# Moving weight tiles by 64 bytes in SBUF: a wider pad at the right-hand edge and an offset inside the low-part tiles

## The chip, the cores and the metric

One core of a Trainium2 chip runs the whole layer in one launch. The time is the device time of one execution in microseconds (us), the median of several runs. Single instructions are in nanoseconds (ns). The engines are PE (TensorE, matmuls), PEld (its weight loads), DVE (VectorE), ACT (ScalarE), POOL (GpSimd) and SP (SyncE, which issues the large DMAs).

## The reference, cut to what matters

The kernel computes one decoder layer in float32 for 256 tokens of width 2048:

```python
h = rmsnorm(x, g_pre_mix)
proj = h @ w_in                                   # 2048 x 15376
oa = gated_deltanet(conv_silu(aq, ak, av), beta, logdecay) -> gated norm
ob = hgrn2(bq, bf, bi) -> gated norm
oc = memory_attention(cq, rmsnorm(mem, g_mem), w_kv_mem)
merged = sum_b sigmoid(gate_b) * (o_b @ w_br_b)
x = x + rmsnorm(merged @ w_out, g_post_mix)
m = square(relu(rmsnorm(x, g_pre_mlp) @ w_mlp_in)) @ w_mlp_out     # 2048 -> 8192 -> 2048
x = x + rmsnorm(m, g_post_mlp)
```

Nearly all of the work is dense products of 256 tokens with large weight matrices, and every weight is read from HBM once.

## The kernel before, in words

**Split products.** PE multiplies in a reduced form of float32 (type fp32r). To keep the accuracy, each operand is split into a high part (the value rounded to fp32r) and a low part (what is left). A product is then high x high, high x low and low x high. ACT makes the high part of a weight tile (`A.copy` into `wh` or `oh`), DVE the low part (a subtraction into `wl` or `ol`); this is `split_w`, lines 204 to 213. Activations are split once and kept: `hh` and `h2h` hold high and low side by side, `memT`, `mgh`/`mgl`, `och`/`ocl`, `mh`/`ml`, `sh`/`sl` likewise.

**A weight tile** is 128 x 2 x 512 elements of 4 bytes (`KG` = 2 blocks of 128 rows, 512 columns), 4096 bytes of each partition. A DMA on SP's queue brings it into a raw tile (`w`, or `raw` in the MLP), and ACT and DVE split it.

**Two ways to multiply.** A matmul has a stationary operand, which a weight load (LDWEIGHTS) brings into the array, and a moving operand, which streams through.

- In `unit` the activations are stationary (128 tokens) and the weights move, 512 columns at a time: three matmuls of 512 columns for each block of 128 rows and each half of the tokens. `first_unit` and the seven products of `seven` work in the same way. In the profile the weights stand first in such rows: `mm<-wh,hh`, `mm<-wl,hh`, `mm<-oh,mh`.
- In `unit_joined` and `unit_stacked` the weights are stationary, 128 columns at a time, and the activations move: for the high weights 512 columns (high and low of 256 tokens side by side), here called wide, and for the low weights 256 columns, here called narrow. `products_joined` issues them: the wide ones of two weight groups, then the narrow ones of the same groups, the order turned from one pair of groups to the next. So runs of wide and narrow follow one another. In the profile the activations stand first: `mm<-hh,wh` and `mm<-h2h,oh` (wide), `mm<-hh,wl` and `mm<-h2h,ol` (narrow).

**Stages.** The mixing stage (memory keys and values, input projection, three branches, output projection) uses both ways. Small steps of the recurrences run in between: `tick` pulls them from a list of generators (`bg`) after each group, so runs of equal matmuls are broken by small ones. The MLP goes over eight blocks `e` of 1024 hidden features: `mlp_in(e)` multiplies with the weights stationary (except the first unit), `mlp_out(e-1)` with the weights moving.

**The order of the work** on an engine is that of the code; the tile framework adds the waits. Nothing in the placement of a tile changes that order, except that a tile waits for the earlier users of the bytes that it takes.

**Where tiles lie.** Pools are laid from the left end of a partition or, with `side="right"`, from the right end. On the left lie the constants, the activations (`hp` and the 4096-byte slots `gp`) and, once the mixing stage is over, the pool `wx` with the MLP's operand pairs 0 and 1 (`oh0`, `ol0`, `oh1`, `ol1`) and `raw0`. On the right lie a pad named `edge`, which no instruction touches, and below it the pool `wp` (four tiles each of `w`, `wh`, `wl`); in the MLP the pool `wy` takes its place with `raw1` to `raw4` and the pairs 2 to 5. The MLP's six operand pairs are a ring: `operand` takes the first of the list and puts it at the end.

In the compiled kernel before, the start addresses are, in bytes within a partition:

```
hh, h2h            18304 + n * 8192    0 modulo 128
gp slots           51072 + n * 4096    0 modulo 128
wx: oh0 ... raw0  155008 + n * 4096    0 modulo 128   (n = 0..4)
wp: w             180160 + n * 4096   64 modulo 128   (n = 0..3)
wp: wh            196544 + n * 4096   64 modulo 128
wp: wl            212928 + n * 4096   64 modulo 128
wy: raw1 ... ol5  180160 + n * 4096   64 modulo 128   (n = 0..11)
```

Slices of these tiles start at multiples of 512 bytes, so the start modulo 128 of a tile is that of all its operands. It is called the phase below.

Of the kernel before, what the change touches and what calls it, by code (L numbers as in the profile page):

```python
# [10 lines left out]
F32 = mybir.dt.float32  # L11
F32R = mybir.dt.float32r
# [5 lines left out]
P = 128  # L18
# [15 lines left out]
KG = 2  # L34
# [6 lines left out]
def tile_trunk(ctx: ExitStack, tc, a):  # L41
# [39 lines left out]
    mk = mixing.enter_context(tc.tile_pool(name="mk", bufs=1))  # L81
    lp = mixing.enter_context(tc.tile_pool(name="lp", bufs=1))
    edge = ctx.enter_context(tc.tile_pool(name="edge", bufs=1, side="right"))
    edge.tile([P, 8], F32, tag="edge", name="edge")
    weights = ctx.enter_context(ExitStack())
    wp = weights.enter_context(tc.tile_pool(name="wp", bufs=4, side="right"))

# [2 lines left out]
    def nm(s):  # L90
        cnt[0] += 1
        return f"{s}_{cnt[0]}"

    def g4(name, shape=(P, 1024), dt=F32):
        return gp.tile(list(shape), dt, tag="g", name=nm(name))
# [99 lines left out]
    def load_w_raw(src, k0, n, c0, width=512, step=None, q=lambda i: i):  # L195
        w = wp.tile([P, KG, 512], F32, tag="w", name=nm("w"), bufs=WB)
        for j in range(0, n, step or n):
            m = min(step or n, n - j)
            q(nc.sync.dma_start(
                w[:, j:j + m, 0:width],  # L200
                src[(k0 + j) * P:(k0 + j + m) * P, c0:c0 + width].rearrange("(k p) n -> p k n", p=P),
            ))
        return w

    def split_w(w, n, width=512, step=None, q=lambda i: i, home=None):
        wh = home("wh") if home else wp.tile([P, KG, 512], F32R, tag="wh", name=nm("wh"))
        wl = home("wl") if home else wp.tile([P, KG, 512], F32R, tag="wl", name=nm("wl"))
        for j in range(0, n, step or n):
            js = slice(j, min(j + (step or n), n))
            q(A.copy(wh[:, js, 0:width], w[:, js, 0:width]))  # L210
            q(V.tensor_tensor(out=wl[:, js, 0:width], in0=w[:, js, 0:width],
                              in1=wh.bitcast(F32)[:, js, 0:width], op=ALU.subtract))
        return wh, wl

    def load_w(src, k0, n, c0, width=512, home=None):
        return split_w(load_w_raw(src, k0, n, c0, width), n, width, home=home)

    def unit(act, nk, src, c0, r0=0, order=None, split=False, post=None, ws=None, load=None):

# [49 lines left out]
    def unit_stacked(pairs, nk, src, c0, ps, load, ws):  # L269

        for gg in range(0, nk // KG, 2):
            groups = []
            for g in (gg, gg + 1):
                k0 = g * KG
                groups.append((k0, ws[g] if g in ws else load(src, k0, c0),
                               [flat(pairs[kt // 4][:, kt % 4]) for kt in range(k0, k0 + KG)]))
            for i, _ in enumerate(products_joined(ps, groups, nk, range(4), gg // 2 % 2)):
                tick(0.5)
# [4 lines left out]
    def unit_joined(both_of, src, c0):  # L283


        out = g4("sum", (P, 4, S))
        tiles, ps, ws = [], [], {}
        for i, (gs, h, turned) in enumerate(halved):
            if i in (0, 1):
                tiles.append(pmm.tile([P, 1024], F32, tag="mm", name=nm("mm")))  # L290
                ps.extend((tiles[-1][:, 0:512], tiles[-1][:, 512:1024]))
            for g in gs:
                if g not in ws:
                    ws[g] = load_w(src, g * KG, KG, c0)
            groups = [(g * KG, ws[g], [flat(both_of(kt)) for kt in range(g * KG, g * KG + KG)]) for g in gs]
            for _ in products_joined(ps, groups, KT, range(4) if h is None else (2 * h, 2 * h + 1), turned):
                tick(0.5 if h is None else 0.25)
            if 7 in gs:
                o = out[:, 2 * h:2 * h + 2, :]
                p = tiles[h].rearrange("p (c s n) -> p c s n", c=2, s=2)  # L300
                A.copy(o, p[:, :, 1, :])
                V.tensor_tensor(out=o, in0=p[:, :, 0, :], in1=o, op=ALU.add)
        return out
# [70 lines left out]
    def first_unit(src, c0):  # L374


        both = pmm.tile([P, 1024], F32, tag="mm", name=nm("mm"))
        ng = KT // KG
        ws, sw = {}, {}

        def fetch(g):
            load_mem(g)
            ws[g] = load_w_raw(src, g * KG, KG, c0, step=1 if g < 2 else None, q=pin)

        def piece(g, js, q=lambda i: i):
            if g not in sw:
                sw[g] = tuple(wp.tile([P, KG, 512], F32R, tag=t, name=nm(t)) for t in ("wh", "wl"))
            wh, wl = sw[g]
            q(A.copy(wh[:, js, :], ws[g][:, js, :]))
            q(V.tensor_tensor(out=wl[:, js, :], in0=ws[g][:, js, :], in1=wh.bitcast(F32)[:, js, :], op=ALU.subtract))  # L390

        def turn(g):
            parts = []
            for kt in (g * KG, g * KG + 1):
                pt, kk = bank("tr"), kt % 4
                for t in range(NT):
                    pin(T.transpose(pt[:, t * P:(t + 1) * P], mem_s[g // 2][:, t, kk * P:(kk + 1) * P], ident))
                parts.append((pt[:, 0:S], *mem_act(kt), gcol[:, kt:kt + 1]))
            return parts

        def products(kt):
            ah, al = mem_act(kt)
            wh, wl = sw[kt // KG]
            j = kt % KG
            ts = [slice(t * P, (t + 1) * P) for t in range(NT)]
            os = [both[:, t * 512:(t + 1) * 512] for t in range(NT)]
            for o, t in zip(os, ts):
                pin(T.matmul(o, ah[:, t], wh[:, j, :], start=kt == 0, stop=False))
                pin(T.matmul(o, al[:, t], wh[:, j, :], start=False, stop=False))
            for o, t in zip(os, ts):  # L410
                pin(T.matmul(o, ah[:, t], wl[:, j, :], start=False, stop=kt == KT - 1))

        fetch(0)
        fetch(1)
        idle_turns(11)
        turn_grow(grow_mem, 16, 0, pin)
        split_scaled(turn(0), pin)
        idle_turns(8)
        for j in range(KG):
            piece(0, slice(j, j + 1), pin)  # L420
        for g in range(ng):
            if 1 <= g < ng - 1:
                piece(g + 1, slice(0, KG))
            if g + 2 < ng:
                fetch(g + 2)
            products(g * KG)
            if g == 0:
                for j, part in enumerate(turn(1)):
                    split_scaled([part], pin)
                    piece(1, slice(j, j + 1), pin)  # L430
            elif g + 1 < ng:
                split_scaled(turn(g + 1))
            products(g * KG + 1)
            if g % 2 == 0 and g > 0:
                sumsq_chunk(mem_s[g // 2 - 1], ssm, g // 2 - 1)
            tick()
        sumsq_chunk(mem_s[3], ssm, 3)
        return both
# [185 lines left out]
    for u in range(2):  # L624
        k = unit_joined(lambda kt: memB[kt // 2][:, kt % 2], w_kv, 512 * u)
# [664 lines left out]
    for hg in range(2):  # L1290
        k, g = forget(unit_joined(hboth, w_in, OFF_BF + 512 * hg), hg)
# [76 lines left out]
    ahead = {}  # L1368

    def first_weights(ps):  # L1370
        for g in range(2):
            ahead[g] = load_w(a["w_mlp_in"][0], g * KG, KG, 0, home=lambda n: g4(n, (P, KG, 512), F32R))

    for c in range(4):
        ys.append(g4("y1", (P, NT, 512)))
# [37 lines left out]
    def at(pool, tag, dt):  # L1413
        return pool.tile([P, KG, 512], dt, tag=tag, name=tag, bufs=1)

    def pair_at(pool, i):
        return (at(pool, f"oh{i}", F32R), at(pool, f"ol{i}", F32R))

    pairs = [pair_at(wx, i) for i in range(2)]
    raws = [at(wx, "raw0", F32)]  # L1420
# [1 line left out]
    def wide_ring():  # L1422
        for g in range(2):
            w = load_w_raw(a["w_mlp_in"][0], g * KG, KG, 512)
            ahead[8 + g] = split_w(w, KG, home=operand)
        weights.close()
        wy = ctx.enter_context(tc.tile_pool(name="wy", bufs=1, side="right", reuse_waits="tile"))
        raws.extend(at(wy, f"raw{i}", F32) for i in range(1, 5))
        raws.append(g4("raw5", (P, KG, 512)))
        pairs.extend(pair_at(wy, i) for i in range(2, 6))  # L1430

    def operand(n):
        if n == "wh":
            pairs.append(pairs.pop(0))
        return pairs[-1][n == "wl"]

    def raw(src, k0, c0):
        w = raws.pop(0)
        raws.append(w)
        nc.sync.dma_start(w, src[k0 * P:(k0 + KG) * P, c0:c0 + 512].rearrange("(k p) n -> p k n", p=P))  # L1440
        return w

    def load_in(src, k0, c0):
        return split_w(raw(src, k0, c0), KG, home=operand)

    h2act = act_of(h2T)
    stf = const("stf", [P, 8])
# [240 lines left out]
```

## Time and profile before

| | |
|---|---|
| median of 3 runs | 1791.68 us (1791.08 to 1791.91) |
| profiled execution, its own time | 1793.1 us |
| span of the profiled execution | 1791.4 us |
| granted TensorE clock | 0.999 |
| PE busy in the span | 1777.5 us, 99% |
| DVE, ACT busy | 1303.3 us (73%), 960.6 us (54%) |
| HBM read | 356.86 MB, mean 203 GB/s moved |

How to read it: matmuls are pipelined, and the profile models their ends. The mean of one matmul (390 to 400 ns at 512 columns) is therefore not the time it adds. What it adds is the distance from its start to the start of the next, here called the pace. In a view in order of time, a row of n equal matmuls gives the start of the first and the time from there to the end of the last.

### The profile page before, as it was taken

What the parts mean: (1) busy time and instruction counts of PE and PEld (TensorE: products, weight loads), DVE (VectorE), ACT (ScalarE), POOL (GpSimd) and SP (SyncE); (2) the same over time, 40 slices, a digit from 0 to 9 for tenths busy, and PEclk for the clock granted to TensorE, in tenths of its full rate; (3) what the DMA queues carried; (4) which work ended last, traced back from release to release, by engine and by line L of the source; (5) the groups of instructions that cost most, each with busy time, mean ns of one, the idle gap of its engine ahead of it and who ended that gap; (6) DMA issues with size and microseconds to landing.
All of it is one profiled execution on the core that took longest, in us unless ns stands there. A gap on an engine that the chain in (4) does not pass through costs nothing.

```text
span 1791.4 us, 23962 instructions
## 1 busy us (share of the span) xinstructions
PE 1777.5 (99%) x9053; PEld 1493.9 (83%) x9053; DVE 1303.3 (73%) x1764; ACT 960.6 (54%) x1217; POOL 57.8 (3%) x100
## 2 busy tenths in 40 slices
PE   9999999999999999999999999999999999999998
PEld 7888888888888888888888888888888878888886
DVE  5765768684758487697555557796979797969795
ACT  6644665454555475565444445665545464645453
POOL 0000000400030000000000000000000000000000
PEclk9999999999999999999999999999999999999999
DMA  8665555875487465555566675776767676767683
GB/s 262 213 191 165 168 159 166 214 215 159 157 213 210 132 189 164 158 171 169 185 186 189 232 222 196 229 243 217 238 222 253 208 242 214 256 200 248 210 296 139
DMA packets 188804, 362.84 MB, mean 203 GB/s; under 512 B 14456, under 2 KB 16272, under 8 KB 188304
## 3 DMA queue, kind: packets, MB, share of 16 engines
q1 hardware_dynamic: 181856, 351.32, 62.0%
q0 software_dynamic: 2304, 5.44, 1.5%
q10 hardware_dynamic: 4528, 4.54, 0.9%
q8 instruction: 71, 1.16, 0.3%
q14 instruction: 45, 0.37, 0.1%
HBM read 356.86 MB, written 4.39 MB: 202 GB/s over the span
## 4 chain that ended last, share of the span: by engine, by line
PE 82%; DVE 2%; issue 1%; ACT 0%; DMA 0%; DVEq 0%; POOLq 0%; POOL 0%
PE mm L56 77%; DVE ol L56 1%; PE pa L56 1%; PE kk L56 0%; DVE relu L56 0%; PE bo L56 0%; PE o L56 0%; DMA raw<-in_w_mlp_out 0%; PE pzt L56 0%; PE pw L56 0%; PE tr L56 0%; DVE raw L56 0%; DVE ml L56 0%; PE y L56 0%; PE mgT L56 0%
## 5 line engine op out<-in xcount | busy, mean ns | idle before, releaser
L56 DVE TENSOR_TENSOR wl<-w,wh 128x1024 fp32r<-128x1024 f32 (+1 forms) x362 | 437.0, 1217 | 245.7 <-ACT wh L56 223.5
L56 ACT CAST wh<-w 128x1024 fp32r<-128x1024 f32 (+1 forms) x362 | 374.6, 1046 | 365.5 <-PE mm L56 296.0
L56 ACT CAST oh<-raw 128x1024 fp32r<-128x1024 f32 x288 | 299.0, 1051 | 283.0 <-PE mm L56 213.0
L56 DVE TENSOR_TENSOR ol<-raw,oh 128x1024 fp32r<-128x1024 f32 x288 | 343.4, 1221 | 100.8 <-ACT oh L56 68.0
L56 PE MATMUL mm<-wh,hh 128*128 128x512 f32 x1152 | 369.2, 395 | 0.0
L56 PEld LDWEIGHTS mm<-wh,hh 128*128 128x128 f32 x1152 | 216.3, 188 | 46.3 <-ACT wh L56 0.2
L56 PE MATMUL mm<-h2h,oh 128*128 128x512 f32 x960 | 228.4, 393 | 0.0
L56 PE MATMUL mm<-wl,hh 128*128 128x512 f32 x576 | 225.5, 392 | 0.0
L56 PEld LDWEIGHTS mm<-h2h,oh 128*128 128x128 f32 x960 | 177.9, 188 | 39.8
L56 PE MATMUL mm<-hh,wh 128*128 128x512 f32 x768 | 188.7, 396 | 0.7 <-ACT z L56 0.7
L56 PEld LDWEIGHTS mm<-hh,wh 128*128 128x128 f32 x768 | 140.7, 188 | 31.5 <-ACT z L56 0.9
L56 PE MATMUL mm<-oh,mh 128*128 128x512 f32 x372 | 146.6, 394 | 0.0
L56 PE MATMUL mm<-ol,mh 128*128 128x512 f32 x372 | 145.3, 391 | 1.1 <-DVE ol L56 1.0
L56 PE MATMUL mm<-oh,ml 128*128 128x512 f32 x372 | 144.9, 392 | 0.0
L56 PEld LDWEIGHTS mm<-wl,hh 128*128 128x128 f32 x576 | 108.3, 188 | 22.7
L56 PEld LDWEIGHTS mm<-h2h,ol 128*128 128x128 f32 x960 | 117.4, 190 | 3.2 <-DVE ol L56 0.6
L56 PE MATMUL mm<-h2h,ol 128*128 128x256 f32 x960 | 118.6, 281 | 0.4 <-DVE ol L56 0.4
L56 PEld LDWEIGHTS mm<-hh,wl 128*128 128x128 f32 x768 | 95.6, 188 | 4.0
L56 PE MATMUL mm<-hh,wl 128*128 128x256 f32 x768 | 98.0, 278 | 0.0
L56 PEld LDWEIGHTS mm<-ol,mh 128*128 128x128 f32 x372 | 69.8, 188 | 18.1 <-DVE ol L56 2.8
L56 PEld LDWEIGHTS mm<-oh,mh 128*128 128x128 f32 x372 | 69.9, 188 | 15.9 <-DVE acc L56 1.4
L56 PEld LDWEIGHTS mm<-oh,ml 128*128 128x128 f32 x372 | 69.8, 188 | 15.7
(363 smaller groups left out, 2212.7 us busy)
## 6 DMA issues: line engine op xcount, KB each, us to landing
w<-in_w_in SPq DMA_DIRECT2D x240, 512.0 KB, 4.2
raw<-in_w_mlp_out SPq DMA_DIRECT2D x170, 512.0 KB, 4.7
raw<-in_w_mlp_in SPq DMA_DIRECT2D x118, 512.0 KB, 4.8
w<-in_w_out SPq DMA_DIRECT2D x32, 512.0 KB, 4.4
w<-in_w_kv_mem SPq DMA_DIRECT2D x30, 512.0 KB, 5.0
w<-in_w_br_c SPq DMA_DIRECT2D x16, 512.0 KB, 3.8
w<-in_w_br_a SPq DMA_DIRECT2D x16, 512.0 KB, 4.5
w<-in_w_br_b SPq DMA_DIRECT2D x16, 512.0 KB, 3.6
```

The costliest lines, as they stand in the source:

```text
L56: ins = op(*args, **kwargs)
```

## The change

Three edits. The pad at the right-hand edge becomes 96 bytes instead of 32, so that everything on the right lies 64 bytes lower. The tiles for the low parts of weights (`wl` in `wp`, `ol0` to `ol5` in the MLP) become 128 bytes longer (32 elements). And a new helper `low` gives the 4096 bytes that are used in such a tile: from its start, or, with `aside=True`, from 64 bytes on. `aside` is set where the weights are stationary (`unit_joined`, and `unit_stacked` with the two groups loaded ahead for it); where the weights move, the low part starts at the tile's start. `home` now gives both tiles in one call, and `operand` turns the ring once for both, as before. No instruction is added or removed.

```diff
-    edge.tile([P, 8], F32, tag="edge", name="edge")
+    edge.tile([P, 24], F32, tag="edge", name="edge")
...
-    def split_w(w, n, width=512, step=None, q=lambda i: i, home=None):
-        wh = home("wh") if home else wp.tile([P, KG, 512], F32R, tag="wh", name=nm("wh"))
-        wl = home("wl") if home else wp.tile([P, KG, 512], F32R, tag="wl", name=nm("wl"))
+    def low(t, aside):
+        o = 16 if aside else 0
+        return t[:, o:o + KG * 512].rearrange("p (k n) -> p k n", k=KG)
+
+    def split_w(w, n, width=512, step=None, q=lambda i: i, home=None, aside=False):
+        if home:
+            wh, wl = home(aside)
+        else:
+            wh = wp.tile([P, KG, 512], F32R, tag="wh", name=nm("wh"))
+            wl = low(wp.tile([P, KG * 512 + 32], F32R, tag="wl", name=nm("wl")), aside)
...
-                groups.append((k0, ws[g] if g in ws else load(src, k0, c0),
+                groups.append((k0, ws[g] if g in ws else load(src, k0, c0, True),
...
-                    ws[g] = load_w(src, g * KG, KG, c0)
+                    ws[g] = load_w(src, g * KG, KG, c0, aside=True)
...
     def pair_at(pool, i):
-        return (at(pool, f"oh{i}", F32R), at(pool, f"ol{i}", F32R))
+        return at(pool, f"oh{i}", F32R), pool.tile([P, KG * 512 + 32], F32R, tag=f"ol{i}", name=f"ol{i}", bufs=1)
...
-            ahead[8 + g] = split_w(w, KG, home=operand)
+            ahead[8 + g] = split_w(w, KG, home=operand, aside=True)
...
-    def operand(n):
-        if n == "wh":
-            pairs.append(pairs.pop(0))
-        return pairs[-1][n == "wl"]
+    def operand(aside):
+        pairs.append(pairs.pop(0))
+        return pairs[-1][0], low(pairs[-1][1], aside)
```

More of the change, by code (lines that the diff above doesn't have):

```diff
@@ L213, in split_w, with load_w @@
         return wh, wl
-    def load_w(src, k0, n, c0, width=512, home=None):
-        return split_w(load_w_raw(src, k0, n, c0, width), n, width, home=home)
+    def load_w(src, k0, n, c0, width=512, home=None, aside=False):
+        return split_w(load_w_raw(src, k0, n, c0, width), n, width, home=home, aside=aside)
     def unit(act, nk, src, c0, r0=0, order=None, split=False, post=None, ws=None, load=None):
@@ L386, in piece @@
             if g not in sw:
-                sw[g] = tuple(wp.tile([P, KG, 512], F32R, tag=t, name=nm(t)) for t in ("wh", "wl"))
+                sw[g] = (wp.tile([P, KG, 512], F32R, tag="wh", name=nm("wh")),
+                         low(wp.tile([P, KG * 512 + 32], F32R, tag="wl", name=nm("wl")), False))
             wh, wl = sw[g]
@@ L1371, in first_weights @@
         for g in range(2):
-            ahead[g] = load_w(a["w_mlp_in"][0], g * KG, KG, 0, home=lambda n: g4(n, (P, KG, 512), F32R))
+            ahead[g] = load_w(a["w_mlp_in"][0], g * KG, KG, 0,
+                              home=lambda aside: tuple(g4(n, (P, KG, 512), F32R) for n in ("wh", "wl")))
     for c in range(4):
@@ L1441, in raw, with load_in @@
         return w
-    def load_in(src, k0, c0):
-        return split_w(raw(src, k0, c0), KG, home=operand)
+    def load_in(src, k0, c0, aside=False):
+        return split_w(raw(src, k0, c0), KG, home=operand, aside=aside)
     h2act = act_of(h2T)
```

## The prediction

> **What bounds the kernel now.** I read the page first: who is busy, and which chain ended last.
>
> ```profile
> span 1791.4 us, 23962 instructions
> PE 1777.5 (99%) x9053; PEld 1493.9 (83%) x9053; DVE 1303.3 (73%) x1764; ACT 960.6 (54%) x1217; POOL 57.8 (3%) x100
> ...
> PE   9999999999999999999999999999999999999998
> ...
> PEclk9999999999999999999999999999999999999999
> ```
>
> PE is busy from end to end at full clock, so the time is the number of matmuls times their pace. The change touches no count, only addresses; the question is whether the pace depends on them. Next I read the groups, for the counts of what reads a weight tile:
>
> ```profile
> L56 PE MATMUL mm<-wh,hh 128*128 128x512 f32 x1152 | 369.2, 395 | 0.0
> L56 PE MATMUL mm<-h2h,oh 128*128 128x512 f32 x960 | 228.4, 393 | 0.0
> L56 PE MATMUL mm<-wl,hh 128*128 128x512 f32 x576 | 225.5, 392 | 0.0
> L56 PE MATMUL mm<-hh,wh 128*128 128x512 f32 x768 | 188.7, 396 | 0.7 <-ACT z L56 0.7
> L56 PE MATMUL mm<-oh,mh 128*128 128x512 f32 x372 | 146.6, 394 | 0.0
> ...
> L56 PE MATMUL mm<-h2h,ol 128*128 128x256 f32 x960 | 118.6, 281 | 0.4 <-DVE ol L56 0.4
> L56 PE MATMUL mm<-hh,wl 128*128 128x256 f32 x768 | 98.0, 278 | 0.0
> ...
> L56 PE MATMUL mm<-oh,sh 128*128 128x512 f32 x112 | 45.0, 402 | 0.1
> ...
> L56 PE MATMUL mm<-memT,wh 128*128 128x512 f32 x128 | 31.7, 398 | 0.0
> ```
>
> The kernel before holds its own comparison. In the MLP, pairs 0 and 1 lie in `wx` at phase 0 (modulo 128 bytes, like the activations), pairs 2 to 5 in `wy` at phase 64, and the ring sends the same work through all six. The view in order of time shows one stretch of `mlp_in`; following the ring through the code, the 32 wide from 1139.72 all use pairs 2 to 5, the first 16 from 1150.93 pairs 0 and 1, the second 16 pairs 2 and 3:
>
> ```profile
> 1139.72 7.63 PE L56 MATMUL mm<-h2h,oh 128*128 128x512 f32 x32
> 1147.19 3.91 PE L56 MATMUL mm<-h2h,ol 128*128 128x256 f32 x32
> 1150.93 7.55 PE L56 MATMUL mm<-h2h,oh 128*128 128x512 f32 x32
> 1158.32 3.93 PE L56 MATMUL mm<-h2h,ol 128*128 128x256 f32 x32
> ```
>
> Wide at phase 64: (1147.19 - 1139.72) / 32 = 233.4 ns. The mixed run takes 1158.32 - 1150.93 = 7.39 us; less 16 x 233.4 ns that leaves 3.66 us, 228.5 ns each, for the 16 at phase 0. The same view cut to short windows gives the two halves apart, and the first eight after the switch:
>
> ```profile
> 1151.17 3.58 PE L56 MATMUL mm<-h2h,oh 128*128 128x512 f32 x15
> ...
> 1154.82 3.66 PE L56 MATMUL mm<-h2h,oh 128*128 128x512 f32 x15
> ...
> 1150.93 2.00 PE L56 MATMUL mm<-h2h,oh 128*128 128x512 f32 x8
> ```
>
> One matmul's modelled length is about 0.39 us here, so the paces are (3.58 - 0.39) / 14 = 228 at phase 0, (3.66 - 0.39) / 14 = 234 at phase 64, and (2.00 - 0.39) / 7 = 230 for the first eight at phase 0. The pace settles after a switch; the later eight of those 16 then take 2 x 228.5 - 230 = 227.
>
> The narrow ones go the other way. In the run from 1147.19 the first 16 use phase 64 and the rest phase 0. Groups in two windows of it:
>
> ```profile
> L56 PE MATMUL mm<-h2h,ol 128*128 128x256 f32 x15 | 1.9, 277 | 0.0
> ...
> L56 PE MATMUL mm<-h2h,ol 128*128 128x256 f32 x15 | 2.0, 283 | 0.0
> ```
>
> A mean lies 162 to 164 ns above the pace (393 in the group of wide ones against 7.39 us / 32 = 231; 281 in that of narrow ones against (1150.93 - 1147.19) / 32 = 117). So 277 is a pace of 114 at phase 64 and 283 one of 120 at phase 0. For the narrow ones a low tile 64 bytes off the activations is better; for the wide ones a high tile in phase with them.
>
> Last, weights moving. In the final `mlp_out` the unit goes 48 matmuls on pairs 2 to 5 and 24 on pairs 0 and 1 in turn. Three rows in order of time (starts of such blocks), and the groups of one window at phase 0 and one at phase 64:
>
> ```profile
> 1738.77 0.40 PE L56 MATMUL mm<-oh,mh 128*128 128x512 f32 x1
> ...
> 1749.77 0.40 PE L56 MATMUL mm<-oh,mh 128*128 128x512 f32 x1
> ...
> 1755.26 0.40 PE L56 MATMUL mm<-oh,mh 128*128 128x512 f32 x1
> ```
>
> ```profile
> L56 PE MATMUL mm<-oh,ml 128*128 128x512 f32 x5 | 2.0, 390 | 0.0
> L56 PE MATMUL mm<-oh,mh 128*128 128x512 f32 x5 | 1.9, 390 | 0.0
> L56 PE MATMUL mm<-ol,mh 128*128 128x512 f32 x5 | 1.9, 389 | 0.0
> ...
> L56 PE MATMUL mm<-oh,mh 128*128 128x512 f32 x14 | 5.5, 394 | 0.0
> L56 PE MATMUL mm<-oh,ml 128*128 128x512 f32 x13 | 5.1, 392 | 0.0
> L56 PE MATMUL mm<-ol,mh 128*128 128x512 f32 x13 | 5.0, 388 | 0.0
> ```
>
> Phase 64: 11.00 us / 48 = 229.2; phase 0: 5.49 us / 24 = 228.8 with the settling in it. Settled, the three means average 389.7 against 391.3, so 1.6 ns by rounded rows; the same 48 and 24, if the first ten of 24 cost 3.5 ns extra as the wide ones do, give 227.3 against 229.2. I take 2 ns.
>
> **The change part by part.** After it, each pool tile's address follows from the sizes: the topmost `wl` moves down 64 bytes for the pad and 128 for its own length, 225216 to 225024, which is 0 modulo 128; a tile of 4224 bytes is 33 x 128, so all `w`, `wh`, `wl`, `raw` and `oh` on the right come to phase 0. `wx` does not move. Low parts with `aside` lie at phase 64.
>
> *Wide, weights stationary, phase 64 to 0.* The ring uses pairs 0 and 1 for 336 of the 960 `h2h,oh`; the other 624 change. In the MLP's runs of 32 a switch is left only at the start: the first 16 at 228.5, the rest at 227, so 227.8 against 233.4: 624 x 5.6 = 3.5 us, and 336 x (228.5 - 227.8) = 0.2 us. In the mixing stage `hh,wh` and `memT,wh`, 768 + 128, have means 396 and 398, a pace of 233 to 235. Their runs are shorter and broken by recurrence steps, where the first eight give only 233.4 - 230 = 3.4. I take 4.5, between 3.4 and 6: 896 x 4.5 = 4.0 us.
>
> *Narrow.* The 336 `h2h,ol` of pairs 0 and 1 go from phase 0 to 64: 120 to 117, 1.0 us. The other 624 + 768 + 128 keep their phase, but they follow a wide run in another rhythm. Phase 64 shows two rhythms, 114 (the 277 above) and (3.93 - 0.28) / 31 = 118 in the run from 1158.32, which is at phase 64 throughout. I take no change for these; were all at 114, 624 x 3 = 1.9 us more, were the mixing stage's (mean 278, pace 115) all at 118, 896 x 3 = 2.7 us less.
>
> *Weights moving, phase 64 to 0.* In the mixing stage and the first MLP unit these are
>
> ```profile
> L56 PE MATMUL mm<-wh,oh 128*128 128x512 f32 x128 | 50.5, 394 | 0.0
> ...
> L56 PE MATMUL mm<-wh,och 128*128 128x512 f32 x64 | 25.4, 397 | 0.0
> ...
> L56 PE MATMUL mm<-wh,memT 128*128 128x512 f32 x128 | 38.6, 399 | 0.8 <-DVE memT L56 0.8
> ```
>
> three rows for each branch and gate product: 1152 + 576 (`hh`), 6 x 128 (`oh`, `mg`), 3 x 64 (`och`), 128 + 64 (`memT`), 2880 in all. At 2 ns, less a tenth for settling after each break: 2880 x 1.8 = 5.2 us. Bounds: 2.3 each (6.6 us) and nothing, if every run is broken before it settles.
>
> *`mlp_out`.* 3 x 372 + 3 x 112 = 1452, two thirds of them, some 970, at phase 64 now: 970 x 2 = 1.9 us, and the 24/48 switching ends. But DVE is nearly full in these stages:
>
> ```profile
> 1218.50:1263.30 44.80, 44.80 (x258) 39.09 (x257) 29.88 (x29) 20.51 (x27) 0.00 (x0) 1.00 0.66 212
> 1263.30:1305.30 42.00, 41.81 (x181) 33.55 (x180) 41.04 (x46) 25.91 (x27) 0.00 (x0) 1.00 0.75 250
> ```
>
> In this row of stages (length, then PE, PEld, DVE, ACT) the `mlp_out` of 42.00 us has 41.04 us of DVE, the `mlp_in` before it 29.88 of 44.80. What PE gains in `mlp_out` can run into DVE's subtraction, which is late next there. I take 1.5 us of 1.9.
>
> *At nothing:* ACT's copies and DVE's subtractions only move by 64 bytes; they are covered by PE except in `mlp_out`. The longer tiles make `wy`'s tiles overlap up to two of `wp`'s instead of one, so pair 2 may wait for one group more of the first MLP unit, 12 x 229 = 2.7 us; but PE reaches it only after four runs on pairs 0 and 1 (2 x 16 x (233 + 120) ns = 11 us), which hide it. Uncovered it would cost those 2.7 us, once. DMA count and sizes stay; its share in these stages is 0.66 and 0.75.
>
> Sum: 3.5 + 0.2 + 4.0 + 1.0 + 5.2 + 1.5 = 15.4 us. The profiled span goes from 1791.4 to 1776.0 us. Its own time is 1793.1, 1.4 above the median of the runs, 1791.68, so the median goes to **1776 us** (0.9% less). Bounds from the terms: most 3.5 + 5.4 + 1.0 + 1.9 + 6.6 + 1.9 + 0.2 = 20.5 (1771), least 3.5 + 3.0 + 1.0 - 2.7 + 0 + 0 = 4.8 (1787).
>
> The Trainium skill (SBUF - State Buffer, "Who interferes with whom") says PE never waits on anyone at SBUF, and (TensorE: Matmul & The Clock Gate, "Part 2: What happens when you issue a matmul") that loading the next weights takes no read bandwidth from the running matmul. By that rule the change is worth nothing. The trace disagrees: the same wide matmul runs at 228 or 234 ns, by the place of its weights.
>
> **The rivals.**
>
> *The place, not the phase (no change, 1791.5 us).* Pairs 0 and 1 also lie in another region, 155008 to 175488, than 2 to 5. If that makes the 5 ns, moving by 64 bytes does nothing but the 336 x 0 to 3 ns of `ol0`, `ol1`. For it: no tile in the trace has one without the other. Against it: wide and narrow prefer opposite pairs, which a region that is simply better would not give. 8%. The skill's rule above ends here too.
>
> *A longer period than 128 bytes (1783 us).* All operands before are at 384 or 448 modulo 512. After, `wh` keeps the known relation (195968 is 384 modulo 512), but the low tiles and pairs 1, 3, 4, 5 fall on 0, 128, 256 as well. If only the known relation is good, three quarters of the 624 and of the `wl` third of 2880, and all of `mlp_out`, win nothing: 15.4 - 2.6 - 1.3 - 1.5, and up to 2.7 more for the narrow: 7 to 10 us gained, 1782 to 1784. 15%.
>
> *The narrow runs lose their cover (slower, 1802 us).* A narrow matmul needs a weight load (mean 188 to 190 ns in the groups) every 117 ns, so loads must overlap, and none has yet been seen at phase 64 behind a wide run at phase 0. If the rhythm that locks in is worse by twice the spread seen (2 x 7 ns), 1856 x 14 = 26 us go against 15.4. It decides from 15.4 us / 1856 = 8.3 ns, a narrow pace of about 125. Against it: 114, 118, 120 are all that appear. 7%.
>
> *More than forecast (1771 us).* All runs settle at once and the narrow ones at 114. 6%.
>
> **How the numbers follow.** Forecast 64%, and the four rivals as given. About 0.2% (3.6 us) is what a measurement of this kernel can tell from no change. Faster by that are the forecast, the longer period and the better case: 85%. Same: 8%. Slower: 7%. The range 1769 to 1787 holds the forecast, the better case and most of the longer period.
>
> **What would show it.** In the changed profile: `h2h,oh` and `hh,wh` means down from 393 and 396 to 389 to 392; no row of `h2h,ol` at 283; `wh,hh` from 395 to 393; 32 wide in 7.3 us instead of 7.47 between starts. Wrong, if these stay (region), if `mlp_out` stages keep their 42 us (DVE), or if the narrow means rise above 288.

## The result and the profile after

| | before | changed |
|---|---|---|
| median of 5 runs | 1791.91 us (1791.08 to 1793.83) | 1783.85 us (1783.16 to 1785.93) |
| ratio | 1 | 0.9956, 95% interval 0.9942 to 0.9971 |
| span of the profiled execution | 1791.4 us | 1781.4 us |

The kernel became faster by 8.1 us in the medians, 10.0 us in the profiled spans: the profiled run before lay 1.2 us above its median, the one after 0.7 us below. The prediction was 1776 us, a sum of 15.4 us. The measured time lies inside the range of 1769 to 1787, but by the medians the gain is half of the forecast. It lies next to the rival *a longer period than 128 bytes* (1782 to 1784 us). Medians and ratios here and below count only executions at a granted clock of 0.998 or 0.999; one of the kernel with low tiles 32 bytes off ran at 0.654, took 2515.97 us and is not counted.

The page of the changed kernel, its groups of matmuls (behind the first bar: busy us, then the mean ns of one):

```profile
span 1781.4 us, 23962 instructions
PE 1767.7 (99%) x9053; PEld 1491.5 (84%) x9053; DVE 1302.8 (73%) x1764; ACT 961.1 (54%) x1217; POOL 57.8 (3%) x100
...
L56 PE MATMUL mm<-wh,hh 128*128 128x512 f32 x1152 | 366.6, 393 | 0.0
...
L56 PE MATMUL mm<-h2h,oh 128*128 128x512 f32 x960 | 227.7, 393 | 0.0
L56 PE MATMUL mm<-wl,hh 128*128 128x512 f32 x576 | 226.1, 392 | 0.0
...
L56 PE MATMUL mm<-hh,wh 128*128 128x512 f32 x768 | 184.8, 392 | 0.7 <-ACT z L56 0.7
...
L56 PE MATMUL mm<-oh,mh 128*128 128x512 f32 x372 | 146.2, 393 | 0.0
...
L56 PE MATMUL mm<-h2h,ol 128*128 128x256 f32 x960 | 114.6, 277 | 0.5 <-DVE ol L56 0.5
...
L56 PE MATMUL mm<-hh,wl 128*128 128x256 f32 x768 | 99.6, 280 | 0.0
```

Still 99% PE and the same 9053 matmuls: nothing but the pace has moved. `hh,wh` fell from 396 to 392 and `wh,hh` from 395 to 393, as forecast. But four rows did not do what was forecast. `h2h,oh` is still at 393 and `wl,hh` still at 392, while the narrow `h2h,ol` fell to 277, the best value that windows of the kernel before had shown, and the narrow `hh,wl` rose from 278 to 280.

Three answers in windows of the changed kernel show what stopped the gain. First, the groups of two neighbouring stretches of one gate product, 1040.6 to 1042.6 and 1043.4 to 1045.3 us:

```profile
L56 PE MATMUL mm<-wl,mgh 128*128 128x512 f32 x4 | 1.6, 395 | 0.0
L56 PE MATMUL mm<-wh,mgh 128*128 128x512 f32 x3 | 1.2, 389 | 0.0
L56 PE MATMUL mm<-wh,mgl 128*128 128x512 f32 x3 | 1.2, 388 | 0.0
...
L56 PE MATMUL mm<-wl,mgh 128*128 128x512 f32 x4 | 1.6, 389 | 0.0
L56 PE MATMUL mm<-wh,mgl 128*128 128x512 f32 x3 | 1.2, 389 | 0.0
L56 PE MATMUL mm<-wh,mgh 128*128 128x512 f32 x3 | 1.2, 389 | 0.0
```

The low tile of the first stretch starts at 216576, which is 0 modulo 256; that of the second at 212352, which is 128 modulo 256. Both are 0 modulo 128. The activations and all `wh` are at 128 modulo 256. So of two low tiles that the prediction held to be equal, one costs 6 ns more (a pace of 234 against 227 between starts), at once and without settling. The same holds over the whole mixing stage, tile by tile, with the addresses of the compiled kernel: moving low tiles that start 128 or 384 bytes off the activations modulo 512 take 233.6 and 233.8 ns, those 256 bytes off 227.2.

The same in the MLP: one run of 32 wide matmuls goes through an even and an odd pair in turn, eight each. Windows on matmuls of an odd pair (pair 5, `oh` at 0 modulo 256, 1124.2 to 1125.4 us) and of an even one (pair 0, 128 modulo 256, 1126 to 1127.2 us), groups:

```profile
L56 PE MATMUL mm<-h2h,oh 128*128 128x512 f32 x7 | 1.8, 395 | 0.0
...
L56 PE MATMUL mm<-h2h,oh 128*128 128x512 f32 x7 | 1.7, 389 | 0.0
```

And the whole run with the narrow one behind it, in order of time:

```profile
1122.04 7.55 PE L56 MATMUL mm<-h2h,oh 128*128 128x512 f32 x32
1129.43 3.80 PE L56 MATMUL mm<-h2h,ol 128*128 128x256 f32 x32
1133.06 1.32 PE L56 MATMUL mm<-h2h,oh 128*128 128x512 f32 x5
```

Wide: (1129.43 - 1122.04) / 32 = 230.9 instead of the forecast 227.8. Narrow: (1133.06 - 1129.43) / 32 = 113.4 instead of 117.

To place the difference I added up, for both traces, the distances from each matmul's start to the next start (those over 300 ns, which hold a wait or a break, left out), by family. The last columns are of the kernel `e3_mod256` below.

| family | matmuls | before, ns each | changed | difference, us | forecast, us | e3 | e3, us |
|---|---|---|---|---|---|---|---|
| wide, mixing | 883 | 233.3 | 228.0 | -4.9 | -4.0 | 227.9 | -4.7 |
| wide, MLP | 960 | 231.7 | 230.9 | -0.8 | -3.7 | 228.6 | -2.9 |
| narrow, mixing | 895 | 116.3 | 118.2 | +1.6 | 0 | 118.2 | +1.6 |
| narrow, MLP | 959 | 118.3 | 113.9 | -4.3 | -1.0 | 118.1 | -0.4 |
| weights moving, mixing and first MLP unit | 2905 | 229.4 | 228.4 | -2.8 | -5.2 | 227.2 | -6.1 |
| weights moving, `mlp_out` | 1432 | 229.8 | 230.7 | +2.2 | -1.5 | 227.1 | -3.9 |

The changes sum to -9.0; the distances over 300 ns in these families gave another 0.9 (39.6 us before, 38.7 after), which makes nearly the 10.0 us of the spans.

### The profile page after: what moved, and what is told of

It is laid out like the page before. It is cut to its first block, busy times and chain, and to the rows that moved or that the text cites. A ratio compares the mean times of both kernels' runs of the same rounds, so it can differ in the third digit from the quotient of the medians.

```text
span 1781.4 us, 23962 instructions
## 1 busy us (share of the span) xinstructions
PE 1767.7 (99%) x9053; PEld 1491.5 (84%) x9053; DVE 1302.8 (73%) x1764; ACT 961.1 (54%) x1217; POOL 57.8 (3%) x100
## 4 chain that ended last, share of the span: by engine, by line
PE 81%; DVE 2%; issue 1%; ACT 1%; DMA 0%; DVEq 0%; POOLq 0%; POOL 0%
PE mm L56 77%; DVE ol L56 1%; PE pa L56 1%; PE kk L56 0%; DMA raw<-in_w_mlp_out 0%; DVE relu L56 0%; PE bo L56 0%; PE o L56 0%; PE pzt L56 0%; PE pw L56 0%; PE tr L56 0%; DVE raw L56 0%; DVE ml L56 0%; PE y L56 0%; PE mgT L56 0%
## 5 line engine op out<-in xcount | busy, mean ns | idle before, releaser
L56 PE MATMUL mm<-hh,wh 128*128 128x512 f32 x768 | 184.8, 392 | 0.7 <-ACT z L56 0.7
L56 PEld LDWEIGHTS mm<-h2h,ol 128*128 128x128 f32 x960 | 113.7, 188 | 3.2 <-DVE ol L56 0.7
L56 PE MATMUL mm<-h2h,ol 128*128 128x256 f32 x960 | 114.6, 277 | 0.5 <-DVE ol L56 0.5
```

Of the source, the lines that this page charges most:

```text
L56: ins = op(*args, **kwargs)
```

## The experiments

Theory A, formed from the trace after: the pace of a matmul goes by the addresses of its two operands modulo 256. Theory B is the prediction's modulo 128. Theory C is that DVE or waits ate the gain, and the rival *the place, not the phase* stands too. In every kernel of this case the activations lie at 128 modulo 256. So no run here tells whether the distance between the two operands counts, or the weight tile's own start modulo 256; theory A is tested as a rule for the weights' addresses beside these activations.

**The pad alone.** The kernel before with `edge.tile([P, 24], ...)` and nothing else. All weight tiles on the right lie at 128 modulo 256.

> The kernel before with the 96-byte pad alone; low tiles keep 4096 bytes, so every weight tile on the right lies at 128 modulo 256, as the activations do. Theory A (pace goes by the addresses modulo 256) and theory B (modulo 128, as the prediction had it) agree here: wide 228, weights moving 227 throughout, narrow 120 to 121. Against the profile before: wide -5 (mixing) and -3 (MLP), weights moving -6 (mixing) and -2.5 (MLP), narrow +2 (MLP) and +4 (mixing) us: about 1781 us. Theory C (what the change lacked was eaten by DVE or by waits, not by addresses): weights moving stay at 228.4 and 230.7, and mlp_out keeps its 42 us.

Measured: 1781.83 us, ratio 0.994 (0.9928 to 0.9953), span 1777.4. Groups:

```profile
L56 PE MATMUL mm<-wl,hh 128*128 128x512 f32 x576 | 224.5, 390 | 0.0
L56 PE MATMUL mm<-h2h,oh 128*128 128x512 f32 x960 | 224.4, 390 | 0.0
...
L56 PE MATMUL mm<-h2h,ol 128*128 128x256 f32 x960 | 120.5, 283 | 0.4 <-DVE ol L56 0.4
L56 PE MATMUL mm<-hh,wl 128*128 128x256 f32 x768 | 101.6, 283 | 0.0
```

Weights moving reached 390 and wide 390, which the change did not reach; the narrow ones sit at 283, the 120 that was expected. The place falls: pairs 2 to 5 did not leave their region, moved by 64 bytes, and their wide matmuls run at 227.5 ns over all 960. C falls as the main cause: with the right addresses, weights moving in `mlp_out` take 227.2 ns. Beside the change's 0.9956 (0.9942 to 0.9971), the pad alone cannot be told from the whole change: in the narrow matmuls the offset of the low parts wins (113.9 against 120.2 ns in the MLP, 118.2 against 120.6 in the mixing stage), and the longer tiles lose it where the weights move (228.4 against 227.2, 230.7 against 227.2 in `mlp_out`) and in the MLP's wide ones (230.9 against 227.5).

**A pad of 224 bytes.** The kernel before with `edge.tile([P, 56], ...)`: everything on the right at 0 modulo 256. This tells A from B.

> The kernel before with a pad of 224 bytes alone: every weight tile on the right lies at 0 modulo 256 (0 modulo 128), the activations stay at 128 modulo 256. B: the same as the 96-byte pad, about 1781 us, weights moving at 227. A: weights moving at 232 to 234 on the right (mixing +9 us against before), wide at 232.6 (no gain), narrow at a relation not seen yet: 1795 to 1802 us, slower than before.

Measured: 1804.68 us, ratio 1.007 (1.0058 to 1.0083), span 1802.7. Slower than before, above A's interval; B, which wanted 1781, falls. Groups:

```profile
L56 PE MATMUL mm<-wh,hh 128*128 128x512 f32 x1152 | 372.1, 397 | 0.0
...
L56 PE MATMUL mm<-wl,hh 128*128 128x512 f32 x576 | 227.4, 395 | 0.0
L56 PE MATMUL mm<-hh,wh 128*128 128x512 f32 x768 | 188.1, 396 | 0.7 <-ACT z L56 0.7
...
L56 PE MATMUL mm<-hh,wl 128*128 128x256 f32 x768 | 101.0, 282 | 0.0
```

128 bytes more of padding than the 96-byte pad, and `wl,hh` goes from 390 to 395. The loss against before lies in weights moving, 232.6 ns against 229.4 in the mixing stage (9.8 us) and 231.6 against 229.8 in `mlp_out` (4.2 us), and in the narrow ones of the mixing stage, 119.9 against 116.3 (3.3 us). A had priced the first of the three alone, so the time came out 3 us above its interval.

**All operands at 128 modulo 256.** The changed kernel, with the high tiles of the MLP's pairs laid together and every second low tile used from 128 bytes on:

```diff
-    def low(t, aside):
-        o = 16 if aside else 0
+    def low_tile():
+        lows[0] += 1
+        return wp.tile([P, KG * 512 + 32], F32R, tag="wl", name=nm("wl")), lows[0] % 2 == 0
+
+    def low(t_odd, aside):
+        t, odd = t_odd
+        o = 16 if aside else 32 if odd else 0
...
-        return at(pool, f"oh{i}", F32R), pool.tile([P, KG * 512 + 32], F32R, tag=f"ol{i}", name=f"ol{i}", bufs=1)
+        his = [at(pool, f"oh{i}", F32R) for i in ids]
+        los = [(pool.tile([P, KG * 512 + 32], F32R, tag=f"ol{i}", name=f"ol{i}", bufs=1), i % 2 == 1) for i in ids]
+        return list(zip(his, los))
```

> The changed kernel with all operands put at 128 modulo 256: in the MLP the high tiles lie together ahead of the low ones, and every second low tile, which starts at 0 modulo 256, is used from 128 bytes on where the weights move (from 64 bytes on where they are stationary, as in the change). A: weights moving 227 everywhere, wide 228 everywhere, narrow as in the changed kernel (114 in the MLP, 118 in mixing): 8 us below the changed kernel, about 1775 us. B: as the changed kernel, 1784 us.

Measured: 1777.39 us, ratio 0.9917 (0.9903 to 0.993), span 1775.2. Its interval lies below that of the change (0.9942 to 0.9971): it beats both the kernel before and the changed one, and it comes within 2 us of what the prediction gave for the change. Every run of it (1776.44 to 1778.58 us) also lies below every run of the pad alone (1779.13 to 1783.67), though the two intervals just touch. It stays 2.4 us above the 1775 that A gave. Groups, and one run of wide and narrow in order of time:

```profile
L56 PE MATMUL mm<-h2h,oh 128*128 128x512 f32 x960 | 225.5, 391 | 0.0
L56 PE MATMUL mm<-wl,hh 128*128 128x512 f32 x576 | 224.5, 390 | 0.0
...
L56 PE MATMUL mm<-h2h,ol 128*128 128x256 f32 x960 | 118.6, 280 | 0.5 <-DVE ol L56 0.5
L56 PE MATMUL mm<-hh,wl 128*128 128x256 f32 x768 | 99.6, 280 | 0.0
```

```profile
1140.99 7.48 PE L56 MATMUL mm<-h2h,oh 128*128 128x512 f32 x32
1148.31 3.93 PE L56 MATMUL mm<-h2h,ol 128*128 128x256 f32 x32
1152.08 1.11 PE L56 MATMUL mm<-h2h,oh 128*128 128x512 f32 x4
```

Weights moving run at 227 everywhere. Wide: 7.32 us / 32 = 228.8. But narrow: 3.77 / 32 = 117.8, where the changed kernel had 113.4. The low tiles stand in the same relation to the activations in both kernels (64 or 192 modulo 256); only the high tiles of the runs in front differ. So the narrow pace depends also on what runs in front of it, and 4 us that the change had won in the MLP by its uneven high tiles went when these were put in phase. Why the narrow ones run faster behind uneven high tiles stays open.

The windows by stage of this kernel and of the changed one, the same `mlp_out` (length, then PE, PEld, DVE, ACT):

```profile
1253.00:1294.60 41.60, 41.37 (x181) 33.54 (x181) 40.59 (x46) 25.89 (x28) 0.00 (x0) 1.00 0.74 253
```

```profile
1255.60:1297.60 42.00, 41.91 (x182) 33.57 (x181) 40.89 (x46) 25.84 (x27) 0.00 (x0) 1.00 0.75 251
```

Over the seven `mlp_out` stages, e3 takes 333.7 us, the change 338.5, the kernel before 337.5. DVE is as full as before and did not forbid the 3.8 us. In the stage shown, 180 matmuls at 226.7 would be 40.8 us, not 41.6. Of the rest, 0.65 us lies in four distances in a row, 617, 338, 264 and 339 ns from 1266.65 us on, the first of which holds a wait of 0.23 us for DVE's `ol`. The kernel before has the same four in its stage from 1263.30 (585, 340, 261 and 339 ns), so what DVE takes there hardly changed.

**Low tiles 128 bytes off.** As e3, with `o = (0 if odd else 32) if aside else ...`: under stationary weights the low tiles lie at 0 modulo 256.

> As the kernel with all operands at 128 modulo 256, but low tiles under stationary weights start at 0 modulo 256, 128 bytes off the activations instead of 64. If narrow matmuls go by the address modulo 128, they take 120 as in phase: 6 to 8 us above that kernel, about 1782 us. If by 256, a pace of its own, 112 to 118, within 3 us of that kernel.

Measured: 1782.28 us, ratio 0.9946 (0.9932 to 0.996). The narrow pace is 120.5 (MLP) and 121.3 (mixing), that of tiles in phase (120.2 and 120.6 with the 96-byte pad). Groups:

```profile
L56 PE MATMUL mm<-h2h,ol 128*128 128x256 f32 x960 | 120.8, 284 | 0.4 <-DVE ol L56 0.4
L56 PE MATMUL mm<-hh,wl 128*128 128x256 f32 x768 | 102.0, 284 | 0.0
```

So for the narrow ones 0 and 128 are alike, while for 512 columns they are 227 and 233 to 234. The two kinds follow different rules.

**32, 96 and 16 bytes off.** As e3, with `o = 8`, `24` and `4` elements instead of 16 for `aside`. The low tiles that start at 0 modulo 256 then lie 160, 224 and 144 bytes off, the others 32, 96 and 16.

> As the kernel with all operands at 128 modulo 256, but low tiles under stationary weights start 32 bytes off the activations instead of 64. If the narrow pace has two levels (in phase 120, off phase 114 to 118), 32 bytes is one of the two: within 4 us of 1777 us. If the narrow pace goes by the distance in bytes, it lies between 118 and 120, 1778 to 1781 us. Everything else as in that kernel: weights moving 227, wide 228.

> As above with 96 bytes instead of 64. By distance in a period of 128 bytes, 96 equals 32: the same narrow pace as the 32-byte kernel, 1778 to 1781 us. By distance in a period of 256 with 128 as bad as 0: nearer to 120 than 64 is. A narrow pace of 114 behind wide runs in phase would give 1769 us.

> As the kernel with all operands at 128 modulo 256, but low tiles under stationary weights start 16 bytes off the activations. If the level changes only at multiples of 64 bytes, this is as in phase: narrow 120, about 1781 us. If any offset breaks the coincidence: narrow 114 to 118, 1770 to 1778 us.

Measured, in the order of the offsets 16, 32 and 96: 1780.85 us (ratio 0.9937, 0.9922 to 0.9952), 1780.34 (0.9935, 0.9918 to 0.9952) and 1777.22 (0.9918, 0.9903 to 0.9932). The narrow pace of MLP and mixing is 119.4 and 119.6, 119.2 and 119.9, 117.6 and 119.1, against 118.1 and 118.2 at 64 bytes. So it is neither two clean levels nor a function of the distance in a period of 128, by which 32 and 96 would be equal. Within the 96-byte kernel the MLP's narrow matmuls take 118 to 119 ns on tiles 96 bytes off and 116 to 117 on tiles 224 off, so 128 bytes more are not always alike. 64 and 96 cannot be told apart in time, 16 and 32 gain little over being in phase, and in none does the mean of a family come to 114 behind wide runs in phase.

**The change without its pad.** `edge.tile([P, 8], ...)` in the changed kernel.

> The change without its wider pad: longer low tiles and the 64-byte offset alone, so high tiles stay 64 bytes off the activations and low tiles under stationary weights come to 0 or 128 modulo 128-byte phase 0. By the addresses: wide on the right stays at 233, narrow there goes from 116 to 120 (mixing +3.5 us, MLP +2 us), weights moving stay at 229: 1796 to 1799 us, slower than before. If the offset of the low tiles helped by itself, below 1791 us.

Measured: 1799.64 us, ratio 1.004 (1.0026 to 1.0054), slower than before, 0.6 us above the expected interval. Groups:

```profile
L56 PE MATMUL mm<-hh,wh 128*128 128x512 f32 x768 | 188.4, 396 | 0.7 <-ACT z L56 0.7
...
L56 PE MATMUL mm<-ol,mh 128*128 128x512 f32 x372 | 146.4, 394 | 1.6 <-DVE ol L56 1.6
...
L56 PE MATMUL mm<-hh,wl 128*128 128x256 f32 x768 | 101.6, 283 | 0.0
```

The wide ones keep the 396 of before, the narrow ones of the mixing stage go to 283 (120.6 ns, 3.8 us). The rest came otherwise than expected: the MLP's narrow ones stayed at 118.4, and the matmuls with weights moving, which were to stay at 229, went to 230.3 (2.6 us) and in `mlp_out` to 231.3 (3.7 us; `ol,mh` from 391 to 394). So the time is near the expected one in part by luck. The longer tiles with their offset are a loss by themselves, and the change gains nothing beyond its pad. The two parts do not add up: alone they make 10.4 us less and 7.1 us more, together 8.1 less; what one is worth depends on the addresses that the other leaves.

## Why the prediction was right and wrong, point by point

- **What bounds the kernel, and that the pace depends on the place of the weights:** right, and the profile after shows it. The Trainium skill (SBUF - State Buffer, "Who interferes with whom") says that PE never waits on anyone. The times here cannot be had from that rule: kernels that differ in addresses alone took from 1777 to 1805 us. Which access waits for which, no run shows.
- **The address step, "all `w`, `wh`, `wl`, `raw` and `oh` on the right come to phase 0", with the phase taken modulo 128:** this is the step that failed. The kernel before had only distances of 0 and 64 bytes in it, so its trace could not tell a period of 128 from 256. With 4224-byte tiles half of the low tiles, and the high tiles of pairs 1, 3 and 5, come to 0 modulo 256, where 512 columns take 233 to 234 instead of 227 ns. (Pair 1 lies in `wx`, which the prediction held still: the longer `ol0` moves `oh1` from 163200 to 163328.) With the same tiles put at 128 modulo 256 (e3), the time fell from 1783.85 to 1777.39 us. The prediction gave a longer period 15%, and its 1782 to 1784 us hold the measured time, in part by luck: it priced three quarters as lost, by a period of 512, where half are, took `mlp_out` at nothing where it lost 2.2 us, and the narrow ones of the MLP gained 3.3 us more than forecast.
- **Wide, mixing:** forecast 4.0 us, measured 4.9. The `wh` tiles did keep the known relation.
- **Wide, MLP:** forecast 3.7, measured 0.8, since every second pair is off (395 against 389 in the windows). In phase it measured 2.9 (e3).
- **Weights moving, mixing:** forecast 5.2, measured 2.8, since half of the `wl` are off; in phase 6.1 (e3). The step of 2 ns was right and the tenth for settling too much. The count of 2880 leaves out the 96 of the first MLP unit (`wh,h2h` and `wl,h2h`), less than 0.2 us.
- **`mlp_out`:** forecast 1.5 us gained, measured 2.2 lost. Pairs 1, 3 and 5 are worse at 0 modulo 256 (232.7 ns) than the tiles that lay 64 bytes off (229.9). The stages did keep their 42 us, one of the prediction's signs of being wrong, but not by its cause. The reason for holding back, DVE's 41.04 of 42.00 us, was not what stopped it: with addresses in phase the matmuls there gained 3.9 us and the seven stages 3.8.
- **Narrow, no change but for pairs 0 and 1:** mis-sized both ways. The MLP gained 4.3 instead of 1.0, with a mean of 113.9 on all pairs; the mixing stage lost 1.6. The two paces, 113.9 and 118.2, are the two rhythms that the prediction named, but the MLP's gain is above its bound of 1.0 + 1.9 us, since pairs 0 and 1 went to 114 and not to 117.
- **Edits at nothing:** the counts stand, and DVE's and ACT's busy times are 1302.8 and 961.1 us against 1303.3 and 960.6. No wait of `wy`'s tiles appeared: the first `mlp_in` took 92.8 us against 93.8.
- **The rivals:** the place falls with the 96-byte pad. The narrow ones did not lose their cover: the worst mean of a family in any kernel is 121.3 ns, where the rival needed 125. The 1771 us of the better case was not reached by any kernel; the lowest median is 1777.22. The range's lower end of 1769 lies 2 us below the 1771 that the terms gave, without a reason.

## What to carry to other kernels

Where PE is busy from end to end, write down the start address of both operands of each hot matmul, modulo 256 at least, before and after an edit of the layout, and look in the old trace for rows that already have the new relation; a tile lengthened by a "harmless" 128 bytes shifts its neighbours by half of that period. A regularity found in a trace is known only at the distances that occur in it: before a modulus is used for new distances, one run with a pad can test it. And test the parts of a change alone, since here one part alone gained 0.6% and the other alone lost 0.4%.

## What was not expected of the hardware

- A matmul of 512 columns with a weight load of its own takes 227 ns from start to start, once settled, where the weight tile's address agrees with the activations' modulo 256, 229 to 233 at 64 bytes off, and 232 to 234 at 128 off; at 256 and 384 modulo 512 the values of 0 and 128 come again (low tiles of the changed kernel: 227.2 and 233.8). The activations lay at 128 modulo 256 throughout, so that it is the distance that counts is not shown.
- 256 columns have another rule: 120 to 121 at 0 and at 128 bytes off in the kernels with 512 columns in phase (118.6 to 119.9 at 128 off with the pad of 224 bytes), 113 to 119 at 64 and 192, and which of these depends also on the run in front.
- At 64 and 192 bytes off, a narrow rhythm lasts for a whole run of 32 (3.63 us in the changed kernel, 3.77 in e3), while the wide pace changes with the tile: seven matmuls of an odd pair and seven of an even one have means of 395 and 389 ns within one run.
